# A hybrid encoder layer: the output projection's steps traced in a fixed order for every engine

## The chip, the core and the metric

The kernel runs on one core of a Trainium2 chip. The metric is device time in microseconds (us) of one execution; lower is better. The engines' short names are those of the profile: PE is TensorE's matmul, PEld its weight load, DVE VectorE, ACT ScalarE, POOL GpSimd, SP SyncE, which issues the DMAs.

## What is computed

One encoder layer on two sequences (1024 and 2048 rows of 1024 numbers, float32). The part that matters here is its end:

```python
u = rms_norm(h, norm_w); proj = u @ w_in
y_f = fourier(...) * silu(z_f)                      # 512 columns
y_s = (ssd_fwd + ssd_bwd + D * xs) * silu(z_s)      # 1536 columns, 4 groups of 384
yg = y_s.reshape(b, s, 4, 384)
yg = yg * rsqrt(mean(yg * yg, -1) + EPS)            # norm of each group
h = h + concatenate([y_f, y_s * ssd_norm_w], -1) @ w_out     # the output projection: 2048 -> 1024
h = h + (p @ w_ple_in) * sigmoid(h @ w_ple_gate)             # the last stage
return rms_norm(h, final_norm_w)
```

## The kernel before

Four stages follow each other: the input projection with the state space part, the Fourier part, the output projection, the last stage. The change is in the output projection (lines 1153 to 1264).

**Steps.** The 3072 rows are 24 chunks of 128 (eight each of the blocks P, S1 and S2), taken two at a time: 12 pairs. The 2048 inputs are split in two passes p of 1024. So there are 24 steps n, pair by pair, first pass 0 and then pass 1; each adds its part to the residual rows, which lie in memory between the passes (Hd). Between the passes, behind step 11, the weights are replaced (`product_weights`, lines 850 to 861: per product one load, four ACT casts, four DVE subtractions).

**One step.** A step multiplies a 2 x 2 arrangement of 128 x 512 blocks by the weights with seven products, in a Strassen-like scheme (P1, P2, P6, P5, P7, P4, P3 in that order, lines 1215 to 1238). Each product is 12 matmuls of 512 columns (line 1104), since each operand is split into a rounded part and a rest, and three of the four combinations count. Its operands A11, A12, S2, S1, S3, A22, S4 are made in `halves` (1066 to 1097): differences s3, s1, s2, s4 on DVE (L1080), the rounded part `ah` on ACT (L1074), the rest `al` on DVE (L1075). The products accumulate in PSUM: X takes P1, then P6, then P7 on top; Y takes P2; Z takes P5, then P3; W takes P4. Between P1 and P6, P6 and P7, and P7 and the next P1, ACT copies X out (`kept`, L1113, tile `pu`, called p1, u2, u3), and the next product on X waits for it. Each output quarter is then added to the residual tile `ht` by DVE out of PSUM (L1218) and by POOL from `pu` (L1219).

**Preparing a step.** The two y tiles of a step are loaded (L1173). For pairs of block S1 (n = 4 to 7 and 16 to 19) a correction comes first: 12 small matmuls `po` (L1185), four DVE multiplications into the tile `big` (L1186), two POOL additions into y (L1190). Then the group norm: ACT squares (L865, tile `sq`, one buffer), POOL sums each half in two additions (L866, L867) into `rs`; ACT rounds `rs` into `sh` (L871), POOL writes the rest (L872), PE sums over the partitions with two matmuls `pb` (L874), ACT takes Ln and Exp, each behind a table load (L875, L876). POOL then scales the two y tiles (L880). y has four buffers, `ht` four, the differences three, `ah` and `al` seven each.

**What sets the order.** The program traces, for every n, the first half of preparing step n + 2 (`prepare`), then the rest of preparing step n + 1, then the products of step n. The scheduler, with its own model of durations, sets from the dependencies which instruction each engine takes next. So the seven products of a step are interleaved with those of its neighbours, and every step has its own order. At run time each engine takes its instructions strictly in the order that was set.

Of the kernel before, what the change touches and what calls it, by code (L numbers as in the profile page):

```python
# [18 lines left out]
P = 128  # L19
# [37 lines left out]
def tile_hybrid_encoder(ctx: ExitStack, tc: tile.TileContext, a):  # L57
# [787 lines left out]
    def weight_tiles(pool, name):  # L845
        return [pool.tile([P, 4, 512], F32R, tag=f"w{x}{name}", name=f"w{x}{name}") for x in "hl"]
# [16 lines left out]
    def squares(y, sq, rs):  # L863

        S.activation(sq, y.rearrange("p (r k) l -> p r k l", r=2)[:, :, 1:4, :], AF.Square)  # L865
        G.tensor_tensor(rs, sq[:, :, 0, :], sq[:, :, 1, :], op=ALU.add)  # L866
        G.tensor_tensor(rs, rs, sq[:, :, 2, :], op=ALU.add)  # L867

    def group_rstd(sh, pb, rs):

        S.copy(sh[:, 0], rs)  # L871
        G.tensor_tensor(sh[:, 1], rs, sh[:, 0].bitcast(F32), op=ALU.subtract)  # L872
        for j in range(2):
            T.matmul(pb, lhsT=ones_r, rhs=sh[:, j], start=(j == 0), stop=(j == 1))  # L874
        S.activation(rs, pb, AF.Ln, bias=eps4, scale=1.0 / 384.0)  # L875
        S.activation(rs, rs, AF.Exp, scale=-0.5)  # L876

    def group_scale(y, rs):
        ssd = y.rearrange("p (r k) l -> p r k l", r=2)[:, :, 1:4, :]
        G.tensor_tensor(ssd, ssd, rs.unsqueeze(2).broadcast_to([P, 2, 3, P]), op=ALU.mult)  # L880

    with ExitStack() as ph:
# [63 lines left out]
        for step, (seq, f) in enumerate(order):  # L946
# [58 lines left out]
            if last:  # L1005
                for q in range(2):
                    pb = fpr.tile([P, 2, P], F32, tag="pm", name="pb")
                    sq = fp.tile([P, 2, 3, P], F32, tag="Uo", bufs=1, name="sq")
                    sh = fp.tile([P, 2, 2, P], F32R, tag="traw", name="sh")
                    rs = fp.tile([P, 2, P], F32, tag="fold0", name="rs")  # L1010
                    squares(y_first[:, q], sq, rs)
                    group_rstd(sh, pb, rs)
                    group_scale(y_first[:, q], rs)

# [84 lines left out]
    def product(ps, A, W, op, name, first=True):  # L1099
        (ah, al), (wh, wl) = A[op], W[name]  # L1100
        i = 0
        for k in range(4):
            for at, wt in ((ah, wh), (ah, wl), (al, wh)):
                T.matmul(ps, lhsT=at[:, k, :], rhs=wt[:, k, :], start=(first and i == 0), stop=(i == 11),  # L1104
                         skip_group_check=not first)
                i += 1
# [45 lines left out]

    with ExitStack() as ph:
        yp = ph.enter_context(tc.tile_pool(name="yp", bufs=1, **R_))
        hbs, behind = [], []
# [6 lines left out]
        def prepare(p, i):  # L1162

            ys, hts, rss = [], [], []
            for q in range(2):
                bi, c = todo[2 * i + q]
                b = BLOCKS[bi]
                tk = slice(c * P, (c + 1) * P)
                if p == 0 and i == 0:
                    y = y_first[:, q]  # L1170
                else:
                    y = yp.tile([P, 8, P], F32, tag="y", bufs=4, name="y")
                    nc.sync.dma_start(y, Yd[bi][:, 8 * p:8 * p + 8, tk])  # L1173
                ys.append(y)
                if b["n"] == "S1":

                    if not behind:
                        behind.append(ox.tile([P, 2, 8, P], F32, tag="big", name="big"))
                    ct, zb = behind[0][:, q, 0:2, :], behind[0][:, q, 2:8, :]
                    nc.sync.dma_start(ct, CTd[:, 2 * p:2 * p + 2, tk])  # L1180
                    nc.sync.dma_start(zb, ZSd[:, 6 * p:6 * p + 6, tk])
                    for g in range(2):
                        po = mps.tile([P, 3, P], F32, tag="sm", bufs=3, name="po")
                        for j in range(3):
                            T.matmul(po[:, j, :], lhsT=hbs[-1][:, 3 * g + j, :], rhs=ct[:, g, :], start=True, stop=True)  # L1185
                        V.tensor_tensor(zb[:, 3 * g:3 * g + 3, :], po, zb[:, 3 * g:3 * g + 3, :], op=ALU.mult)  # L1186
            for q in range(2):
                if BLOCKS[todo[2 * i + q][0]]["n"] == "S1":
                    ssd = ys[q].rearrange("p (r k) l -> p r k l", r=2)[:, :, 1:4, :]
                    G.tensor_tensor(ssd, ssd, behind[0][:, q, 2:8, :].rearrange("p (r k) l -> p r k l", r=2), op=ALU.add)  # L1190
                if p == 0 and i == 0:
                    continue
                if q == 0:
                    rs = yp.tile([P, 4, P], F32, tag="rs", bufs=2, name="rs")
                rss.append(rs[:, 2 * q:2 * q + 2])
                sq = yp.tile([P, 2, 3, P], F32, tag="sq", bufs=1, name="sq")
                squares(ys[q], sq, rss[q])
            if rss:
                sh = yp.tile([P, 2, 4, P], F32R, tag="sh", bufs=1, name="sh")
                pb = mps.tile([P, 4, P], F32, tag="sm", bufs=3, name="pb")  # L1200
                group_rstd(sh, pb, rs)

            def rest():
                for q in range(2):
                    if rss:
                        group_scale(ys[q], rss[q])
                    bi, c = todo[2 * i + q]
                    b = BLOCKS[bi]
                    r0 = b["t0"] + c * P
                    hts.append(residual(Hd[bi * NCH + c] if p else a["x"][b["seq"]][r0:r0 + P, :]))  # L1210
                quarter = lambda q, r: (lambda: ys[q][:, 4 * r:4 * r + 4, :])
                return halves(quarter(0, 0), quarter(0, 1), quarter(1, 0), quarter(1, 1)), hts
            return rest

        def outputs(i, W, A, hts):
            def add(q, ns, ps):
                h = hts[q][:, ns]
                V.tensor_tensor(h, ps, h, op=ALU.add)  # L1218
                return lambda t: G.tensor_tensor(h, h, t, op=ALU.add)  # L1219

            X, Y, Z, X2 = bank("X"), bank("Y"), bank("Z"), bank("W", bufs=2)
            product(X, A, W, "A11", "P1")
            p1 = kept(X)
            product(Y, A, W, "A12", "P2")
            add(0, N0, Y)(p1)
            product(X, A, W, "S2", "P6", first=False)
            u2 = kept(X)
            product(Z, A, W, "S1", "P5")
            more = add(1, N1, Z)
            product(X, A, W, "S3", "P7", first=False)  # L1230
            u3 = kept(X)
            more(u3)
            product(X2, A, W, "A22", "P4")
            add(1, N0, X2)(u3)
            product(Z, A, W, "S4", "P3", first=False)
            add(0, N1, Z)(u2)
            for q, (bi, c) in enumerate(todo[2 * i:2 * i + 2]):
                nc.sync.dma_start(Hd[bi * NCH + c], hts[q])

        ready = prepare(0, 0)()  # L1240
        ld = product_weights(0, NAMES[3:4], W)
        with tc.issue_after(ld.ins):
            coming = prepare(0, 1)
        ld = product_weights(0, NAMES[4:], W)
        with tc.issue_after(ld.ins):
            incoming(0)
        steps = [(p, i) for p in range(2) for i in range(NP)]
        for n, (p, i) in enumerate(steps):
            cur, after = ready, coming
            with tc.issue_after(ld.ins):  # L1250
                if n + 2 < len(steps):
                    if steps[n + 2] == (1, 0):
                        incoming(1)
                    coming = prepare(*steps[n + 2])
                if n + 1 < len(steps):
                    ready = after()
                else:
                    ph.close()
                    q4 = ctx.enter_context(tc.tile_pool(name="q4", bufs=1, **R_))
                    ready = turned(0)  # L1260
            outputs(i, W, *cur)
            if i == NP - 1:
                W = {}
                last_w = product_weights(p + 1, NAMES, W)


    wph = ox.tile([P, 2, DM], F32R, tag="big", name="wph")
# [123 lines left out]
```

## Time and profile before

| | us |
|---|---|
| median of 3 runs (2935.85 to 2945.36) | 2937.86 |
| the profiled execution | 2937.68 |
| its span | 2935.9 |
| PE busy in the span | 2806.0 (96%) |
| DVE, ACT, POOL busy | 2148.7, 1454.0, 1497.0 |
| output projection, first matmul | 2015.5 |
| last stage, first product | 2593.2 |

A PE row counts as busy until its modelled end, and matmuls overlap; how full PE is shows in the idle time before its rows and in the distance between their starts. "PEclk" is the clock that PE was granted, 1.00 being full speed. In a row of the timeline, the number in brackets is the idle time of the engine before it, and behind the arrow is what ended it.

### The profile page before, as it was taken

The page shows a single profiled execution, that of the slowest core. Times are in us where ns is not written, and L with a number is a line of the kernel's source. Part 1 is how long each engine was busy: PE and PEld are TensorE (multiplying, and loading weights), DVE is VectorE, ACT ScalarE, POOL GpSimd, SP SyncE. Part 2 cuts the span into 40 slices and gives each one's busy share as a digit, 9 for nine tenths or more (in the row PEclk, how much of TensorE's full clock was granted, in tenths as well). Part 3 has the DMA queues.
Part 4 walks back from the last instruction along what each step waited for, and adds up shares of the span by engine and source line. Part 5 has one row for each costly group of instructions (what it writes and reads, how often), then busy time and mean ns, then how long its engine had stood idle before and what let it go on. Part 6 is the DMA issues. An engine that isn't in the chain of part 4 may idle for free.

```text
span 2935.9 us, 46306 instructions
## 1 busy us (share of the span) xinstructions
PE 2806.0 (96%) x17206; PEld 2550.2 (87%) x17206; DVE 2148.7 (73%) x3364; ACT 1454.0 (50%) x3008; POOL 1497.0 (51%) x1091
## 2 busy tenths in 40 slices
PE   6999999999999999999999999788998899989998
PEld 6999999999999999999999999776776677768887
DVE  3787777687778686778787776796767876776665
ACT  4545465443545564445444444345555645555554
POOL 1255656542567777643656655455777577610000
PEclk9999999999999999999999999889999999999999
DMA  3244565462465665544455554466453654451221
GB/s 96 88 146 150 166 187 166 125 185 79 127 192 165 200 189 159 160 123 117 144 161 157 154 159 132 151 231 227 144 173 127 229 167 141 158 198 67 96 96 63
DMA packets 327997, 440.09 MB, mean 150 GB/s; under 512 B 19824, under 2 KB 250932, under 8 KB 323932
## 3 DMA queue, kind: packets, MB, share of 16 engines
q1 hardware_dynamic: 327484, 436.08, 47.1%
q8 instruction: 136, 2.23, 0.3%
q10 hardware_dynamic: 288, 1.05, 0.1%
q14 instruction: 89, 0.73, 0.1%
HBM read 328.41 MB, written 109.71 MB: 149 GB/s over the span
## 4 chain that ended last, share of the span: by engine, by line
PE 73%; DVE 7%; POOL 6%; issue 5%; DMA 5%; ACT 4%; SPq 0%; POOLq 0%; DVEq 0%; ACTq 0%
PE ps L361 41%; PE X L1104 7%; PE Z L1104 4%; PE po L648 4%; PE pst L606 3%; PE pd L574 3%; PE W L1297 2%; PE Y L1104 2%; DMA y<-Yd 2%; PE ptt L421 1%; DVE s L1080 1%; DVE al L1075 1%; PE W L1104 1%; PE pr L1028 1%; POOL wl L190 1%
## 5 line engine op out<-in xcount | busy, mean ns | idle before, releaser
L361 PE MATMUL ps<-uh,wh 128*128 128x342 f32 (+1 forms) x2880 | 955.8, 332 | 11.4 <-ACT uh L267 8.2
L361 PE MATMUL ps<-ul,wh 128*128 128x342 f32 (+1 forms) x2880 | 920.6, 320 | 2.5 <-DVE ul L268 2.5
L361 PE MATMUL ps<-uh,wl 128*128 128x342 f32 (+1 forms) x2880 | 922.2, 320 | 0.4 <-POOL wl L190 0.4
L190 POOL TENSOR_TENSOR wl<-wr,wh 128x1024 fp32r<-128x1024 f32 x120 | 296.4, 2470 | 659.3 <-ACT wh L189 658.1
L361 PEld LDWEIGHTS ps<-uh,wh 128*128 128x128 f32 x2880 | 545.6, 189 | 35.0 <-issue 15.8
L361 PEld LDWEIGHTS ps<-ul,wh 128*128 128x128 f32 x2880 | 548.5, 190 | 4.2 <-DVE ul L268 3.5
L361 PEld LDWEIGHTS ps<-uh,wl 128*128 128x128 f32 x2880 | 545.1, 189 | 1.2 <-POOL wl L190 1.1
L558 ACT ACTIVATE R<-R,lb 128x128 f32<-128x128 f32 x1152 | 352.8, 392 | 16.9 <-POOL R L549 16.9
L549 POOL TENSOR_SCALAR_AFFINE_SELECT R<-R 128x512 f32<-128x512 f32 x288 | 275.7, 980 | 6.8 <-DMA R<-ROWd 6.8
L586 POOL TENSOR_TENSOR xw<-xm,wd 128x512 f32<-128x512 f32 x144 | 189.5, 1327 | 136.3 <-ACT xm L423 110.8
L617 DVE SCALAR_TENSOR_TENSOR H<-H,cd,pst 128x64 f32<-128x64 f32 x888 | 182.6, 274 | 102.2 <-PE pst L606 100.0
L367 ACT COPY raw<-ps 128x342 f32<-128x342 f32 x180 | 79.1, 439 | 340.6 <-PE ps L361 339.7
L1104 PE MATMUL X<-whP,ah 128*128 128x512 f32 x480 | 196.7, 410 | 14.1 <-ACT pu L1113 8.4
L402 DVE SCALAR_TENSOR_TENSOR xT<-raw,cvt,xT 128x1024 f32<-128x1024 f32 x144 | 195.5, 1358 | 2.6
L1104 PE MATMUL X<-wlP,ah 128*128 128x512 f32 x480 | 194.5, 405 | 1.6 <-DVE wlP L859 1.6
L1104 PE MATMUL X<-whP,al 128*128 128x512 f32 x480 | 193.6, 403 | 2.4 <-DVE al L1075 2.4
L1219 POOL TENSOR_TENSOR ht<-ht,pu 128x512 f32<-128x512 f32 x96 | 150.4, 1578 | 72.3 <-ACT pu L1113 46.6
L652 DVE TENSOR_TENSOR y<-y,yt 128x512 f32<-128x512 f32 (+1 forms) x144 | 161.4, 1121 | 5.0
L272 ACT ACTIVATE zT<-ps 128x342 f32<-128x342 f32 (+1 forms) x108 | 49.1, 455 | 220.7 <-PE ps L361 220.4
L1075 DVE TENSOR_TENSOR al<-s,ah 128x512 fp32r<-128x512 f32 x144 | 137.7, 981 | 26.5 <-ACT ah L1074 26.0
L565 DVE TENSOR_TENSOR R<-R,cb 128x512 f32<-128x512 f32 x144 | 148.5, 1031 | 5.0
L651 DVE TENSOR_TENSOR yt<-po,er 128x512 f32<-128x512 f32 (+1 forms) x144 | 91.2, 633 | 75.9 <-PE po L648 67.7
(266 smaller groups left out, 5772.8 us busy)
## 6 DMA issues: line engine op xcount, KB each, us to landing
R<-ROWd SPq DMA_DIRECT2D x144, 512.0 KB
wr<-in_w_in SPq DMA_DIRECT2D x120, 512.0 KB
er<-EXPd SPq DMA_DIRECT2D x144, 256.0 KB
Hd<-ht SPq DMA_DIRECT2D x48, 512.0 KB
ht<-Hd SPq DMA_DIRECT2D x48, 512.0 KB
y<-Yd SPq DMA_DIRECT2D x46, 512.0 KB
wlP<-WSd SPq DMA_DIRECT2D x21, 1024.0 KB
Yd<-y SPq DMA_DIRECT2D x72, 256.0 KB
```

Of the source, the lines that this page charges most:

```text
L190: G.tensor_tensor(wl, raw, wh.bitcast(F32), op=ALU.subtract)
L361: T.matmul(ps[:, :n], lhsT=wt[:, kt, :], rhs=ut[:, kt, :n], start=(i == 0), stop=(i == 3 * KT - 1))
L402: V.scalar_tensor_tensor(dst, raw[:, k:k + TB], cvt[:, 20 * k + ct:20 * k + ct + 1], dst, op0=ALU.mult, op1=ALU.add)
L549: G.affine_select(out=R, in_=R, pattern=[[0, 2], [0, 2], [sgn, P]], compare_op=ALU.is_ge, fill=NEG, base=0, channel_multiplier=-sgn)
L558: S.activation(R[:, h, d, c, :], R[:, h, d, c, :], AF.Exp, bias=self.B.lb[:, 2 * p + c, hc + h:hc + h + 1])
L565: V.tensor_tensor(E[0], E[0], cb.unsqueeze(1).broadcast_to([P, 2, 2 * P]), op=ALU.mult)
L586: G.tensor_tensor(xw, self.xm[c4].rearrange("p c (h e) -> p c h e", h=2), col(self.B.wd[:, c4:c4 + 4, hc:hc + 2]).broadcast_to([P, 4, 2, 6 ...
L617: V.scalar_tensor_tensor(dst[:, e], H[d][:, cc, e], B.cd[:, cc, hc + h:hc + h + 1], pst[:, c, e], op0=ALU.mult, op1=ALU.add)
L652: V.tensor_tensor(y[:, cr], y[:, cr], t[:, cr], op=ALU.add)
L1075: V.tensor_tensor(al, src, ah.bitcast(F32), op=ALU.subtract)
L1104: T.matmul(ps, lhsT=at[:, k, :], rhs=wt[:, k, :], start=(first and i == 0), stop=(i == 11), skip_group_check=not first)
L1219: return lambda t: G.tensor_tensor(h, h, t, op=ALU.add)
```

## The change

The output projection's loop is written as a class `Step` with small pieces (load, correct, square, sum, root, scale, each operand, each addition, store), and a function `run(n)` that traces the pieces of three steps at once: the products of step n (`c`), the operands of step n + 1 (`d`), the correction and squares of step n + 2 (`e`), and the store of step n - 1 (`b`). Steps 1 to 22 are traced under `tc.manual_schedule()`, in which the order of every engine and of the DMA queue is the order of the text. Step 0 and step 23 are left to the scheduler. `group_rstd` is split: its ACT rounding and POOL subtraction become `group_parts`. The new weights between the passes are asked for and split inside step 11's text, product by product. Every engine has the same instructions as before, each as often; only their order differs.

```diff
-        ready = prepare(0, 0)()
...
-        for n, (p, i) in enumerate(steps):
-            cur, after = ready, coming
-            with tc.issue_after(ld.ins):
...
-                    coming = prepare(*steps[n + 2])
-                if n + 1 < len(steps):
-                    ready = after()
...
-            outputs(i, W, *cur)
+        def run(n, newer=None):
+            c = all_[n]
+            b = all_[n - 1] if n else None
+            d = all_[n + 1] if n + 1 < len(steps) else None
+            e = all_[n + 2] if n + 2 < len(steps) else None
...
+            c.operand(6)
+            product(X, c.A, W_, "A11", "P1")
+            if d is not None and not d.first and n:
+                d.rooted()
             p1 = kept(X)
+            if e is not None:
...
+                e.rows()
+            if d is not None:
+                d.scaled(0)
+                d.scaled(1)
+            product(Y, c.A, W_, "A12", "P2")
+            asked(0)
+            c.add(0, N0, Y)
+            c.plus(0, N0, p1)
+            if b is not None:
+                b.stored()
+            product(X, c.A, W_, "S2", "P6", first=False)
+            asked(1)
             u2 = kept(X)
+            if d is not None:
+                d.operand(0)
+            product(Z, c.A, W_, "S1", "P5")
+            asked(2)
+            c.add(1, N1, Z)
+            if d is not None:
+                d.operand(1)
+                d.operand(2)
+            if e is not None:
+                e.correct(0)
+            parted(0)
+            product(X, c.A, W_, "S3", "P7", first=False)
+            asked(3)
             u3 = kept(X)
+            c.plus(1, N1, u3)
+            if e is not None:
+                e.correct(1)
+                e.squared(0)
+            if d is not None:
+                d.operand(3)
+            parted(1)
+            product(X2, c.A, W_, "A22", "P4")
+            asked(4)
+            c.add(1, N0, X2)
+            c.plus(1, N0, u3)
+            if d is not None:
+                d.residuals()
+                d.operand(4)
+            if e is not None:
+                e.squared(1)
+            parted(2)
+            product(Z, c.A, W_, "S4", "P3", first=False)
+            asked(5)
+            c.add(0, N1, Z)
+            if e is not None:
+                e.summed()
+            if d is not None:
+                d.operand(5)
+            c.plus(0, N1, u2)
+            parted(3)
+            if newer is not None:
+                asked(6)
+                for k in range(4, 7):
+                    parted(k)
...
+        with tc.manual_schedule():
+            for n in range(1, len(steps) - 1):
+                run(n, newer=W if n == NP - 1 else None)
```

`rooted` is the two pb matmuls, Ln and Exp; `summed` is the ACT and POOL parts of `sh`. `operand(k)` makes, for k = 0 to 6: A11 and s3; s1 and A12; s2 and S2; S1; S3; A22; s4 and S4. `asked` and `parted` do something in step 11 alone. Behind `two` stand, as before, `S.copy(ah, src)` and then DVE's subtraction into `al`.

Three places show what moves. First ACT, around the Ln and Exp of a step of the first pass, before; the three casts from s tiles are S2, S1 and S3, the cast of y is A22, and the last is S4:

```order
L871 CAST sh<-rs 128x512
L1074 CAST ah<-s_22983 128x512
L1074 CAST ah<-s_22981 128x512
L1074 CAST ah<-s_22979 128x512
L1113 COPY pu<-X 128x512
L875 ACT_TABLE_LOAD
L875 ACTIVATE rs<-pb,eps_117 128x512
L1074 CAST ah<-y 128x512
L876 ACT_TABLE_LOAD
L876 ACTIVATE rs<-rs 128x512
L865 ACTIVATE sq<-y 128x768
L1074 CAST ah<-s_23005 128x512
```

and ACT of the change, from the second squares of step n + 2 over the step's end; the cast of y behind `sh` is A22, that of s_22944 is S4, both of step n + 1:

```order
L865 ACTIVATE sq<-y 128x768
L870 CAST sh<-rs 128x512
L1238 CAST ah<-y 128x512
L1238 CAST ah<-s_22944 128x512
L877 ACT_TABLE_LOAD
L877 ACTIVATE rs<-pb,eps_117 128x512
L878 ACT_TABLE_LOAD
L878 ACTIVATE rs<-rs 128x512
L1116 COPY pu<-X 128x512 x2
L1238 CAST ah<-y 128x512 x2
L1238 CAST ah<-s_23030 128x512
L1116 COPY pu<-X 128x512
```

Ln stood ahead of the casts of A22 and S4 and now stands behind both; the copy of X (p1, the first of the `x2`) stands behind Exp; the copy u3 (the last row) stands behind the cast of S2.

Second DVE, a step of the second pass before, from the addition of P4 (W) over that of P3 (Z) to P2's of the next step (Y); s_24836 and s_24834 are s2 and s1, s_24858 is s4:

```order
L1218 TENSOR_TENSOR ht<-W,ht 128x512
L1075 TENSOR_TENSOR al<-y,ah 128x512
L1218 TENSOR_TENSOR ht<-Z,ht 128x512
L1075 TENSOR_TENSOR al<-s_24836,ah 128x512
L1075 TENSOR_TENSOR al<-s_24834,ah 128x512
L1080 TENSOR_TENSOR s_24858<-y,s_24836 128x512
L1218 TENSOR_TENSOR ht<-Y,ht 128x512
```

and of the change, the whole stretch from P5's addition (first row) to P2's of the next step; s_24881, s_24887, s_24866 and s_24968 are s1, s2, s3 and s4:

```order
L1266 TENSOR_TENSOR ht<-Z,ht 128x512
L1232 TENSOR_TENSOR s_24881<-y 128x512
L1239 TENSOR_TENSOR al<-y,ah 128x512
L1232 TENSOR_TENSOR s_24887<-s_24881,y 128x512
L1239 TENSOR_TENSOR al<-s_24887,ah 128x512
L1239 TENSOR_TENSOR al<-s_24881,ah 128x512
L1266 TENSOR_TENSOR ht<-W,ht 128x512
L1239 TENSOR_TENSOR al<-s_24866,ah 128x512
L1266 TENSOR_TENSOR ht<-Z,ht 128x512
L1239 TENSOR_TENSOR al<-y,ah 128x512
L1232 TENSOR_TENSOR s_24968<-y,s_24887 128x512
L1239 TENSOR_TENSOR al<-s_24968,ah 128x512
```

The differences s1 and s2 now stand behind P5's addition, and s4 behind P3's addition and the rest of A22.

Third POOL in a step whose step n + 2 needs the correction, before:

```order
L1219 TENSOR_TENSOR ht<-ht,pu 128x512 x2
L880 TENSOR_TENSOR y<-y,rs 128x2x384 x2
L1190 TENSOR_TENSOR y<-y,big 128x2x384
L1219 TENSOR_TENSOR ht<-ht,pu 128x512
L866 TENSOR_TENSOR rs<-sq 128x256
L867 TENSOR_TENSOR rs<-rs,sq 128x256
L1190 TENSOR_TENSOR y<-y,big 128x2x384
L1219 TENSOR_TENSOR ht<-ht,pu 128x512
L866 TENSOR_TENSOR rs<-sq 128x256
L867 TENSOR_TENSOR rs<-rs,sq 128x256
L872 TENSOR_TENSOR sh<-rs,sh 128x512
```

and in the change:

```order
L882 TENSOR_TENSOR y<-y,rs 128x2x384 x2
L1270 TENSOR_TENSOR ht<-ht,pu 128x512
L1203 TENSOR_TENSOR y<-y,big 128x2x384
L1270 TENSOR_TENSOR ht<-ht,pu 128x512
L1203 TENSOR_TENSOR y<-y,big 128x2x384
L866 TENSOR_TENSOR rs<-sq 128x256
L867 TENSOR_TENSOR rs<-rs,sq 128x256
L1270 TENSOR_TENSOR ht<-ht,pu 128x512
L866 TENSOR_TENSOR rs<-sq 128x256
L867 TENSOR_TENSOR rs<-rs,sq 128x256
L871 TENSOR_TENSOR sh<-rs,sh 128x512
L1270 TENSOR_TENSOR ht<-ht,pu 128x512
```

Both corrections now stand with the addition of u3 between them ahead of all the sums; before, the first half's sums stood between them.

More of the change, by code (lines that the diff above doesn't have):

```diff
@@ L1187, in prepare @@
[L1187 to L1192, printed above, removed]
+                    self.ys.append(y)
+                    if self.corrected:
+                        if q == 0:
+                            self.big = ox.tile([P, 2, 8, P], F32, tag="big", name="big")
+                        nc.sync.dma_start(self.big[:, q, 0:2, :], CTd[:, 2 * p:2 * p + 2, tk])
+                        nc.sync.dma_start(self.big[:, q, 2:8, :], ZSd[:, 6 * p:6 * p + 6, tk])
@@ L1230, in outputs @@
-            product(X, A, W, "S3", "P7", first=False)
-            u3 = kept(X)
[L1232 to L1238, printed above, removed]
-        ready = prepare(0, 0)()
+            if e is not None:
+                if steps[n + 2] == (1, 0):
+                    incoming(1)
+                e.rows()
```

198 lines of the change are left out of this document (138 added, 60 removed).

## Prediction, made before the changed kernel was run

> **What bounds the kernel now.** I first read the busy time of the output projection against that of the last stage. Columns: length, then busy time of PE, PEld, DVE, ACT and POOL with their counts, granted clock, DMA share, GB/s.
>
> ```profile
> 2016.00:2592.00 576.00, 531.12 (x2257) 414.19 (x2255) 429.80 (x452) 302.44 (x463) 397.45 (x275) 0.97 0.53 179
> 2600.00:2900.00 300.00, 298.98 (x1405) 242.78 (x1403) 191.87 (x309) 159.89 (x310) 0.00 (x0) 1.00 0.24 82
> ```
>
> The last stage is full; the projection has 45 us without a matmul and a lower clock. Next, what a full PE would need, from the first and the last row of P1 of step 0 and the rows of W, the tile of P4:
>
> ```profile
> 2015.51 0.39 PE L1104 MATMUL X<-whP,ah 128*128 128x512 f32 x1
> ...
> 2018.30 0.39 PE L1104 MATMUL Y<-whP,ah 128*128 128x512 f32 x1
> ```
> ```profile
> L1104 PE MATMUL W<-whP,ah x96: 390/396/737, 2037.4 to 2570.4; 128*128 128x512 f32 x96
> ```
>
> Twelve matmuls take 2.79 us, 0.2325 each. A step has 84 and two for pb: 20.0 us; with the correction's 12 small ones about 20.7. From the first W row to the last are 23 steps and most of a product, 533 us: about 23.0 us a step. So some 3 us a step is lost, near 65 in all. The chain of waits names what for:
>
> ```profile
> PE X L1104 <- ACT pu L1113: 8.4, 5, 3.3
> PE Z L1104 <- DVE ht L1218: 7.8, 4, 3.7
> PE W L1104 <- ACT ah L1074: 7.7, 6, 2.9
> PE X L1104 <- ACT ah L1074: 5.7, 3, 3.0
> PE Y L1104 <- DVE al L1075: 4.8, 5, 3.5
> ```
>
> (total us, times, longest): no one cause, but operands and copies that come late now and then. And waits cost twice:
>
> ```profile
> 2182.83 0.39 PE L1104 MATMUL Z<-whP,al 128*128 128x512 f32 x1
> 2185.65 0.50 PE L1104 MATMUL X<-whP,ah 128*128 128x512 f32 x1 [2.43 <-ACT pu L1113]
> ```
> ```profile
> 2186.50:2189.80 3.30, 3.30 (x9) 2.56 (x8) 2.08 (x2) 1.14 (x2) 3.30 (x3) 0.50 0.02 5
> ```
>
> After 2.43 us idle, PE had half its clock for 3.3 us, 1.65 us of work lost.
>
> **What the change does to the path.** Nothing is removed or added; it is all order. The gain to be had is those 65 us. What it may cost is seen by following the new order round one step, from P6's start to the next P6's start: each link below is the next instruction that must end first, by data or by its engine's queue. Durations (shortest/median/longest ns) of the links:
>
> ```profile
> L1219 POOL TENSOR_TENSOR ht<-ht,pu x96: 1270/1715/1801, 2026.3 to 2591.9; 128x512 f32<-128x512 f32 x96
> L866 POOL TENSOR_TENSOR rs<-sq x46: 718/747/1243, 2028.2 to 2532.9; 128x256 f32<-128x256 f32 x46
> L867 POOL TENSOR_TENSOR rs<-rs,sq x46: 731/1069/1199, 2029.1 to 2533.7; 128x256 f32<-128x256 f32 x46
> L1190 POOL TENSOR_TENSOR y<-y,big x16: 1832/2018/2310, 2091.2 to 2444.4; 128x768 f32<-128x768 f32 x16
> L1075 DVE TENSOR_TENSOR al<-s,ah x96: 674/693/2893, 2017.0 to 2568.7; 128x512 fp32r<-128x512 f32 x96
> L1075 DVE TENSOR_TENSOR al<-y,ah x69: 674/1081/2337, 2047.3 to 2563.8; 128x512 fp32r<-128x512 f32 x69
> L1080 DVE TENSOR_TENSOR s<-y x46: 677/1227/2336, 2050.1 to 2548.5; 128x512 f32<-128x512 f32 x46
> L1080 DVE TENSOR_TENSOR s<-s,y x23: 681/693/1820, 2053.0 to 2550.4; 128x512 f32<-128x512 f32 x23
> L1080 DVE TENSOR_TENSOR s<-y,s x23: 676/1665/1787, 2056.2 to 2558.4; 128x512 f32<-128x512 f32 x23
> L1186 DVE TENSOR_TENSOR big<-po,big x32: 540/545/559, 2070.9 to 2439.9; 128x384 f32<-128x384 f32 x32
> L1218 DVE TENSOR_TENSOR ht<-Z,ht x48: 673/678/693, 2032.3 to 2580.3; 128x512 f32<-128x512 f32 x48
> L1074 ACT CAST ah<-s x95: 600/617/628, 2015.4 to 2567.7; 128x512 fp32r<-128x512 f32 x95
> ```
>
> ACT's own run of them stands in the timeline of before, with POOL's part of sh:
>
> ```profile
> 2128.20 0.62 ACT L871 CAST sh<-rs 128x512 fp32r<-128x512 f32 x1
> 2128.73 0.58 ACT L1113 COPY pu<-X 128x512 f32<-128x512 f32 x1
> 2129.33 1.28 ACT L875 ACT_TABLE_LOAD   x1
> 2131.43 0.69 ACT L875 ACTIVATE rs<-pb,eps 128x512 f32<-128x512 f32 x1 [0.82 <-PE pb L874]
> 2132.14 1.28 ACT L876 ACT_TABLE_LOAD   x1
> 2133.43 0.63 ACT L876 ACTIVATE rs<-rs 128x512 f32<-128x512 f32 x1
> ```
> ```profile
> 2128.90 1.58 POOL L872 TENSOR_TENSOR sh<-rs,sh 128x512 fp32r<-128x512 f32 x1 [0.73 <-ACT sh L871]
> ```
>
> POOL began 0.08 us after ACT's 2128.82: I take 0.08 per hand-over.
>
> 1. P6 and P5: 24 x 0.2325 and the last one's end, 5.8.
> 2. DVE: P5's addition, s1, the rest of A12, s2. POOL has done its scaling and p1's addition by then and stands still, so the shortest rows: 0.67 + 0.68 + 0.67 + 0.68 = 2.7. With all medians 3.7.
> 3. ACT: cast of S2, then the copy u3, which stands behind it: 0.62 + 0.58 = 1.2.
> 4. POOL: u3's addition, sums of the first half, u3's second addition, sums of the second half. Shortest 2 x 1.27 + 2 x 1.45 = 5.4, medians 2 x 1.72 + 2 x 1.82 = 7.1. DVE's rests of S1 and S3 lie beside the first three; I take 6.3.
> 5. ACT: sh, cast of A22: 1.2.
> 6. DVE: rest of A22, s4. POOL's sh and u2's addition lie beside both, so the medians 1.08 + 1.67 = 2.75; shortest 1.35.
> 7. ACT: cast of S4 0.62, table load 1.28, Ln to Exp's end 2.63, copy p1 0.58: 5.1. Then P6.
>
> With seven hand-overs (0.5) the ring takes **25.6 us**, at shortest 23.2, with all medians 27.2: longer than PE's 20.0 by 5.6, and longer than the 23.0 of before. PE waits twice in it: at the second pb, behind POOL's sh (sh is there 18.2 us after P6's start, the 72 matmuls to pb take 16.7: 1.4), and at P6 behind p1 (4.2). P2 is all that PE has to do meanwhile.
>
> In the eight steps that correct step n + 2 (n = 2 to 5, 14 to 17), link 3 is followed by the rest of S2 (0.69), two multiplications into big (1.09) and the first correction (1.85) instead of the copy (0.58), and POOL has the second correction (2.0) in its queue ahead of the sums: 5.1 more, **30.7**; shortest 28.0, medians and longest about 33.
>
> The clock: a wait of 4.2 us is longer than those above, so P6 and P5, which are in the ring, would run at half clock for a while: up to 1.65 more per ring. Part of such a window may fall on P7, where PE has slack; I take half, 0.85: 26.4 and 31.5.
>
> The Trainium skill ("TensorE: Matmul & The Clock Gate", section "What's actually happening") has the clock halve only after an idle window of about 3.4 us. The rows above show it after 2.43. For the wait of 4.2 both say the same. With the shortest durations the wait at P6 is about 2.7: by the page the clock then stays and the result is the low end below; by the rows it halves and the result is some 35 us above that end.
>
> Step 11 puts new weights into the same queues: four casts ahead of u3 (2.5) and 16 between the casts of A22 and S4 (9.9): 25.6 + 12.4 = 38. The loads themselves are covered if they land within that time.
>
> DMAs, by the chain that ended last (start, length):
>
> ```profile
> 2058.54 5.98 DMA y<-Yd
> ...
> 2259.18 4.27 DMA y<-Yd
> ```
>
> y of step n + 2 is asked for when s4 of step n has been read, near Ln, and squared 13 us later at the earliest; its waits before are of 4 to 6 us, so I cost that at nothing. A later landing would lengthen link 4.
>
> Sum. Rings run from P6 of step 1 to P6 of step 22: 21, of which 8 with correction, one with weights, 12 plain: 12 x 26.4 + 8 x 31.5 + 38 = 607 us.
>
> ```profile
> 2058.64 0.40 PE L1104 MATMUL X<-whP,ah 128*128 128x512 f32 x1
> ...
> 2593.17 0.79 PE L1104 MATMUL X<-whP,ah 128*128 128x512 f32 x1 [1.14 <-ACT ah L1074]
> ```
>
> Before, P6 of step 1 began at 2058.6. In step 1 Ln already stands behind S4's cast; I put P6 5 us later (0 to 8), at 2064. Behind P6 of step 22 come 60 + 84 matmuls, 33.5 us, and about 2 of waits. The last stage's first product: 2064 + 607 + 35 = 2706, against 2593.2. The last stage is full and stays as it is. So +113 us on the profiled 2937.7 (0.2 under the median): **3050**. With the shortest rows and full clock: 12 x 23.2 + 8 x 28.0 + 33 = 535, from 2059: 2627, +34, 2972. With medians and 1.65 everywhere: 12 x 28.8 + 8 x 34.6 + 42 = 664, from 2066: 2766, +173, 3111.
>
> **Rivals.** *Forecast*, rings with collisions and some half clock: 3010 to 3110, 0.52. *Lock-step without collisions*: in a fixed order DVE and POOL settle so that they rarely meet, and the clock stays: 2970 to 3010, 0.29. For it: long idle times of POOL in a long ring. Against: links 4 and 6 have the other engine's work beside them by the order itself. *Slower still*, a y load that lands late or two half-clock windows per step: above 3110, 0.11.
>
> *Faster*: the ring doesn't close, since the table load and Ln get to ACT before S4's cast is due; then PE alone paces a step. Place: link 7. It decides from a ring of 20.9 downward (20.0 and 0.9 for P6 behind Ln, Exp and p1 alone, 3.8 after pb against P2's 2.8). Then 12 x 20.9 + 8 x 21.6 + 33 = 457, and 2059 + 457 + 34 = 2550: -43, 2895. For it: PE's waits of before all come from such accidents of order. Against: ACT's queue as written, and 23.2 as the shortest ring. 0.05. *Nothing to measure*: the rings come out at 23.5 or so on average, what before takes: 0.03; the corrections' 28.0 speak against it.
>
> **How the numbers follow.** 3050 is the forecast's middle. From 2970 to 3105 lie the forecast, the lock-step case and both ends of the unknown durations, 0.8. A measurement of this kernel can tell about 0.3% (9 us) from no change: faster 0.05, same 0.03, slower 0.92.
>
> **What would show it.** Right: PE's waits led by X behind ACT's pu, some 4 us in each of 22 steps, then pb behind POOL's sh; W rows 26 to 27 us apart, 31 in steps 3 to 6 and 15 to 18; half-clock windows about once a step; the last stage's first product near 2706. Wrong: W rows under 23 apart; pu waits under 1 us; POOL waiting on DMA for y; the loss lying in the last stage or in step 12 alone.

## The result, and the profile after

The changed kernel takes 3062.52 us (median of 4 runs, 3060.26 to 3065.62) against 2939.33 for the kernel before: a ratio of 1.0426 (95% interval 1.0412 to 1.044). It is slower by 123 us; 3050 was predicted. The profiled execution took 3065.62 with a span of 3063.8.

The busy time by stage, in the columns of the prediction's first fence (length; PE, PEld, DVE, ACT, POOL; granted clock, DMA share, GB/s):

```profile
2016.00:2718.00 702.00, 573.61 (x2260) 442.58 (x2261) 346.58 (x442) 297.37 (x451) 364.40 (x272) 0.90 0.43 144
2720.00:3020.00 300.00, 294.66 (x1370) 238.02 (x1369) 198.52 (x319) 164.13 (x317) 6.29 (x3) 1.00 0.29 100
```

The output projection, which took 576 us, takes 702 with the same instructions, and its clock went from 0.97 to 0.90. DVE and POOL are busy for less time than before (346.6 for 429.8, 364.4 for 397.5). PE's rows take longer at the lower clock (573.6 for 531.1), but most of the loss is standing still: 128 us without a matmul, where it was 45. The waits of PE in that stage (total us, times, longest):

```profile
PE X L1107 <- ACT pu L1116: 77.0, 21, 11.0
PE pb L876 <- ACT sh L870: 25.1, 10, 5.6
PE pb L876 <- POOL sh L871: 18.3, 22, 0.9
```

Instead of many causes with a few waits each there are now three places. Two return step by step: pb waits for POOL's sh in all of the 22 steps traced in the fixed order, and P6 waits for the copy in 21 of them: 4.07 or 4.08 us at the end of a plain ring, 11.0 at the new weights, but only 1.4 to 2.7 at the end of a ring with a correction. The third, pb behind ACT's sh, is 1.7 us in each of the eight correcting steps and 5.6 twice, in step 1 and at the new weights. One plain step as each engine ran it: PE first, from one P6 to the next, then the links in the order of the prediction (DVE, ACT, POOL, ACT, DVE, ACT).

```profile
2244.58 0.50 PE L1107 MATMUL X<-whP,ah 128*128 128x512 f32 x1 [4.07 <-ACT pu L1116]
...
2264.34 0.50 PE L876 MATMUL pb<-sh,ones_r 128*128 128x512 f32 x1 [0.85 <-POOL sh L871]
...
2271.71 0.50 PE L1107 MATMUL X<-whP,ah 128*128 128x512 f32 x1 [4.08 <-ACT pu L1116]
```
```profile
2252.03 0.69 DVE L1266 TENSOR_TENSOR ht<-Z,ht 128x512 f32<-128x512 f32 x1 [0.37 <-PE Z L1107]
...
2253.84 0.69 DVE L1232 TENSOR_TENSOR s<-s,y 128x512 f32<-128x512 f32 x1
```
```profile
2254.56 0.62 ACT L1238 CAST ah<-s 128x512 fp32r<-128x512 f32 x1 [3.70 <-DVE s L1232]
2255.08 0.58 ACT L1116 COPY pu<-X 128x512 f32<-128x512 f32 x1
```
```profile
2255.74 1.32 POOL L1270 TENSOR_TENSOR ht<-ht,pu 128x512 f32<-128x512 f32 x1 [6.77 <-ACT pu L1116]
2257.02 1.22 POOL L866 TENSOR_TENSOR rs<-sq 128x256 f32<-128x256 f32 x1
2258.31 1.20 POOL L867 TENSOR_TENSOR rs<-rs,sq 128x256 f32<-128x256 f32 x1
2259.47 1.30 POOL L1270 TENSOR_TENSOR ht<-ht,pu 128x512 f32<-128x512 f32 x1
2260.72 0.75 POOL L866 TENSOR_TENSOR rs<-sq 128x256 f32<-128x256 f32 x1
2261.55 0.74 POOL L867 TENSOR_TENSOR rs<-rs,sq 128x256 f32<-128x256 f32 x1
```
```profile
2262.32 0.62 ACT L870 CAST sh<-rs 128x512 fp32r<-128x512 f32 x1 [1.93 <-POOL rs L867]
2262.85 0.61 ACT L1238 CAST ah<-y 128x512 fp32r<-128x512 f32 x1
2266.62 0.62 ACT L1238 CAST ah<-s 128x512 fp32r<-128x512 f32 x1 [3.16 <-DVE s L1232]
2267.26 1.28 ACT L877 ACT_TABLE_LOAD   x1
...
2271.09 0.57 ACT L1116 COPY pu<-X 128x512 f32<-128x512 f32 x1
```
```profile
2263.50 1.34 DVE L1239 TENSOR_TENSOR al<-y,ah 128x512 fp32r<-128x512 f32 x1 [2.38 <-ACT ah L1238]
2264.76 1.77 DVE L1232 TENSOR_TENSOR s<-y,s 128x512 f32<-128x512 f32 x1
```

Each link begins within 0.1 us of the end of the link before, and the last row releases the next P6: 27.13 us from P6 to P6. The waits of 0.85 and 4.08 are PE's two places. The clock behind the long wait, as a window of the same columns:

```profile
2246.00:2248.00 2.00, 2.00 (x6) 1.52 (x6) 0.00 (x0) 0.00 (x0) 2.00 (x2) 0.50 0.38 104
```

### The profile page after: what moved, and what is told of

The parts are those of the page before. It is cut to its first block, busy times and chain, and to the rows that moved or that the text cites. A ratio compares the mean times of both kernels' runs of the same rounds, so it can differ in the third digit from the quotient of the medians.

```text
span 3063.8 us, 46116 instructions
## 1 busy us (share of the span) xinstructions
PE 2849.1 (93%) x17206; PEld 2578.8 (84%) x17206; DVE 2073.1 (68%) x3364; ACT 1454.4 (47%) x3008; POOL 1469.0 (48%) x1091
## 5 line engine op out<-in xcount | busy, mean ns | idle before, releaser
L1107 PE MATMUL X<-whP,ah 128*128 128x512 f32 x480 | 206.4, 430 | 79.2 <-ACT pu L1116 77.6
L1239 DVE TENSOR_TENSOR al<-y,ah 128x512 fp32r<-128x512 f32 x69 | 63.2, 917 | 232.9 <-ACT ah L1238 232.9
L1107 PE MATMUL X<-wlP,ah 128*128 128x512 f32 x480 | 202.4, 422 | 1.5 <-DVE wlP L859 1.5
L1107 PE MATMUL X<-whP,al 128*128 128x512 f32 x480 | 201.6, 420 | 0.9 <-DVE al L1239 0.9
L1270 POOL TENSOR_TENSOR ht<-ht,pu 128x512 f32<-128x512 f32 x96 | 139.3, 1452 | 124.6 <-ACT pu L1116 97.3
L1107 PEld LDWEIGHTS X<-whP,ah 128*128 128x128 f32 x480 | 96.8, 202 | 112.6 <-ACT pu L1116 88.3
```

## The experiments

All are edits of the changed kernel. The first nine were run once each; the kernel before, on the same chips, took 2933.1 us (beside the first four), 2938.4 (the next three) and 2939.4 (the two behind them). The theory is the prediction's ring. The rivals are that PE's own pace with the half clock sets the step, that the other engines do, by their own work or by slowing each other, or that the loss has nothing to do with the order.

### S4's cast late

```diff
-            c.operand(6)
             product(X, c.A, W_, "A11", "P1")
...
             p1 = kept(X)
+            c.operand(6)
```

> The change with one piece of text moved: s4 and the operand S4 are made behind the copy p1 instead of ahead of P1, so that on ACT Ln no longer stands behind S4's cast. Theory (one ring through all queues, closed at ACT by A22's cast, s4, S4's cast, table load, Ln, Exp, p1, P6): in the change's trace sh ends 18.4 us after P6's start; Ln then waits only for the second pb matmul, 1.9 us after sh, and P6 comes at 18.4 + 1.9 + 2.6 + 0.6 = 23.6 after the last P6; both PE waits fall under 1.8 us, so the half-clock window should go too: 22.0 to 23.7 a plain step against 27.1, 26.5 to 28.3 a correcting one against 30.8. Total 2962 to 2997 us. Rival 1 (POOL's chain from u3 to sh, with pb behind it, is the limit, and where Ln stands is of no matter): 27 us a step as before, 3045 or more. Rival 2 (any order fixed by hand loses the interleaving of the products, whatever its details): 3040 or more.

2968.62 us, 94 us less than the changed kernel (88 when each is set against the kernel before on its own chip), within the theory's interval. The waits of PE in the stage:

```profile
PE pb L876 <- ACT sh L870: 28.1, 10, 7.6
PE pb L876 <- POOL sh L871: 18.4, 22, 0.9
PE X L1107 <- ACT pu L1116: 10.9, 13, 6.0
```

The wait for the copy fell from 77.0 us to 10.9, and the other two stayed. A plain step takes 21.90 us (W rows at 2250.95 and 2272.85), with no half clock in it. So the ring was closed through links 6 and 7.

### PE kept busy in the wait

14 matmuls of 512 columns into a PSUM tile that nobody reads are put behind P2 in nine plain steps: extra work, in time that PE otherwise waits.

```diff
...
+                for k in range(14):
+                    T.matmul(idle, lhsT=c.A["A12"][0][:, k % 4, :], rhs=W_["P2"][0][:, k % 4, :], start=True, stop=True)
             product(X, c.A, W_, "S2", "P6", first=False)
```

> The change with 14 more matmuls of 512 columns between P2 and P6 in the plain steps 7 to 10, 12, 13 and 19 to 21, into a PSUM tile that nothing reads. They fill 3.3 us of the 4.07 us that PE waits there. Theory: the wait stays where it is, but PE keeps its full clock, so that the ring with P6 and P5 in it gets 1.65 us shorter: 25.5 us from step to step in eight of those steps (all but 12) instead of 27.1, and about 13 us less in all, 3050, although PE does more. Rival (the half clock is only a sign of the waits and lies in slack, or more matmuls ahead of P6 delay it): 27.1 or more a step, 3062 to 3070.

3052.17 us, the span 13.4 us below that of the changed kernel, though PE does more. Of these, 4.5 us lie ahead of the first step (first W row at 2035.04 for 2039.55) and have nothing to do with the filling; from the first to the last W row it is 663.0 us for 671.5. P6's first row, and the first of P7 24 matmuls later:

```profile
2241.64 0.50 PE L1107 MATMUL X<-whP,ah 128*128 128x512 f32 x1 [0.81 <-ACT pu L1116]
...
2247.34 0.39 PE L1107 MATMUL X<-whP,ah 128*128 128x512 f32 x1
```

P6 and P5 take 5.70 us here. In the changed kernel P7 begins at 2251.83, 7.25 after P6. The 1.55 between them is the half clock, and eight of the nine filled steps (all but the one behind the new weights) take 25.57 us, less by as much than the 27.11 of a plain step in the changed kernel. They make 13 us together; the other steps took 4.6 more. So P6 and P5 are in the ring, and the half clock falls on them in full.

### The same text, ordered by the scheduler

```diff
-        with tc.manual_schedule():
-            for n in range(1, len(steps) - 1):
...
+        for n in range(1, len(steps) - 1):
```

> The change's new text without the fixed order: steps 1 to 22 go through the scheduler as step 0 does. Theory (the loss is in the order that was fixed, not in the new pieces): the scheduler finds its way round the ring as in the kernel before, 23 us a step, 2920 to 2965 in all, with no wait of P6 behind p1 that comes back in every step. Rival 3 (the order of the text, as the scheduler's priority, or the pieces themselves, are what costs): 3000 or more.

2959.19 us, within the interval expected: some 100 of the 123 us are the fixed order's. It is still 26 above the kernel before on that chip. One row of its waits tells of some of that:

```profile
PE Z L1107 <- ACT whP L858: 9.9, 1, 9.9
```

In the kernel before this wait for the first weights is 2.0 us in two times; so the other text costs 8 us in step 0 alone. Another 14.6 lie between the first and the last W row (542.7 us for 528.1 before); at which waits was not followed up.

### The copy p1 ahead of the rooted sums

```diff
+            p1 = kept(X)
             if d is not None and not d.first and n:
                 d.rooted()
-            p1 = kept(X)
```

> The change with two pieces of text swapped: the copy p1 stands ahead of pb, Ln and Exp on ACT. Theory: p1 then waits for S4's cast alone, the table loads, Ln and Exp leave the ring at P6 (3.9 us), but Exp now comes 3.8 us after P6 instead of ahead of it, and the scaling, s3 and P5's addition move back: P6 to P6 by 24.0 us, or 25.2 if the longer wait at pb halves the clock under P2. Correcting steps about 28.5 against 30.8. Total 2990 to 3030 us. Rival 1 (POOL's chain with pb behind it): pb stays where it is, 27 us a step, 3050 or more. Should PE's waits have nothing to do with ACT's queue: 3062.

3032.26 us, 2 above the interval given, nearer to the theory than to the rival, but a smaller gain than expected. Ln and Exp no longer stand ahead of P6, so P6 starts on time; but they have left one ring for another. ACT's and DVE's rows:

```profile
2262.26 0.63 ACT L878 ACTIVATE rs<-rs 128x512 f32<-128x512 f32 x1
...
2264.84 1.14 ACT L1238 CAST ah<-y 128x512 fp32r<-128x512 f32 x2 [1.00 <-POOL y L882]
...
2287.65 0.63 ACT L878 ACTIVATE rs<-rs 128x512 f32<-128x512 f32 x1
```
```profile
2265.50 1.68 DVE L1239 TENSOR_TENSOR al<-y,ah 128x512 fp32r<-128x512 f32 x1 [4.35 <-ACT ah L1238]
2267.10 1.78 DVE L1232 TENSOR_TENSOR s<-y 128x512 f32<-128x512 f32 x1
2268.80 0.68 DVE L1266 TENSOR_TENSOR ht<-Z,ht 128x512 f32<-128x512 f32 x1
```

P5's addition (ht<-Z) has no idle time ahead of it any more: it stands behind A11's rest and s3, which wait for the scaling, which waits for Exp. From Exp to Exp 25.4 us: the ring is closed through the scaling instead of through P6 and P5, and it is about as long.

### u3's second addition late

```diff
             c.add(1, N0, X2)
-            c.plus(1, N0, u3)
...
                 d.operand(5)
+            c.plus(1, N0, u3)
             c.plus(0, N1, u2)
```

> u3's second addition on POOL is moved behind the parts of the sums (its first one stays). Theory (the ring of seven links sets the step): link 4 loses one addition of 1.3 us, so a plain step goes from 27.1 us to 25.8 and a correcting one loses as much; 21 steps by 1.3 us are 27 us, so some 3035 us (3025 to 3045) where the kernel before takes 2939. The waits of P6 behind the copy p1 in the plain steps shrink from 4.07 to about 2.8 us. Rival (POOL has time to spare, and the casts on ACT or the share of the memory port set the step by themselves): the addition only changes its place, 3055 us or more, the waits stay at 4.07.

3066.48 us: the expectation failed. The rival's number came out, and so did its sign: the waits of P6 stayed at 4.08 us, and the one at pb fell from 0.85 to 0.67. But the rows give another reason than its time to spare on POOL. ACT's and POOL's rows of the second half of the squares:

```profile
2260.17 0.85 ACT L865 ACTIVATE sq<-y 128x768 f32<-128x768 f32 x1 [2.12 <-POOL rs L867]
```
```profile
2261.09 0.74 POOL L866 TENSOR_TENSOR rs<-sq 128x256 f32<-128x256 f32 x1 [0.96 <-ACT sq L865]
```

`sq` has one buffer, so ACT can square the second half only when POOL has summed the first, and POOL needs that square next. The addition of 1.30 us had covered that round trip of 0.96. Without it POOL waits, and link 4 is only 0.3 shorter; the steps take 26.9, or 27.5 where a little more half clock falls on them. This reading is from the trace; a second `sq` buffer, which would test it, wasn't tried.

### A22's cast ahead of the sums' cast

```diff
+            if d is not None:
+                d.operand(5)
             if e is not None:
                 e.summed()
-            if d is not None:
-                d.operand(5)
```

> Two calls swapped: A22's cast and its rest stand ahead of the sums' cast sh, everything else as in the changed kernel, S4 at its place ahead of P1 too. Theory (the ring): link 6 and A22's cast, 3.03 and 0.62 us, leave the ring, because VectorE can then make the rest of A22 and s4 while ScalarE waits for POOL's sums; the wait of P6 falls from 4.07 us to under 1, and with it the half clock of 1.65 us a step: 27.1 less 3.65 less 1.65 is 21.8 us a plain step, as with S4 late, so some 2975 us (2962 to 3005). Rival (that S4 stands ahead of p1 on ScalarE is what costs, wherever A22 stands): the wait stays above 3 us, 3040 us or more.

2978.67 us, with plain steps of 22.24 us: within the theory's interval, 84 us gained by one swap of two neighbours. S4 stands at its place ahead of P1; what counted was that DVE's 3 us stood between POOL's sums and Ln.

### The order redone, in three goes

First go: y is asked for ahead of P1, p1 and S4's cast stand ahead of the rooted sums, s4's difference is made a step earlier, A22 ahead of the sums' cast, u3's second addition late, the last three weights' casts spread over the next step (in this and the next two diffs the `if` lines and smaller moves are left out).

```diff
+            e.rows()
             product(X, c.A, W_, "A11", "P1")
             p1 = kept(X)
...
+            c.operand(6)
...
             d.rooted()
...
             d.operand(5)
+            d.last()
             e.summed()
             c.plus(1, N0, u3)
```

> All of the order redone by the ring's reading, still fixed by the program: y asked for first; behind P1 the copy p1, then S4's cast (its difference made at the end of the step before) and then the rooted sums; half of the squares ahead of P7; A22's cast and s4 ahead of the sums' cast, u3's second addition behind it; the new weights' last four parts spread over the next step. Theory (nothing but the chain of engines from one P6 to the next held PE; without it a step is PE's own 20.0 us and the two products of pb): 20.5 us in a plain step, 22 to 23 in a correcting one, some 6 us lost at the weights: 490 us for the 23 steps where the kernel before takes 508, so some 2918 us (2895 to 2940). Rival (the engines beside PE slow each other so much in any order that a step can't come under e1's 21.9 us): 2960 us or more.

2964.09 us: 46 more than expected. Plain steps take 21.76 us each, 1.3 more than expected. The larger part of the 46, some 33 us, lies in the eight correcting steps, which take 24.4 to 28.8 us where 22 to 23 were expected, with PE waiting 1.6 to 1.8 us at pb in each; what makes sh late there was not worked out. The ACT rows of a plain step show what sets that one:

```profile
2242.70 1.14 ACT L1238 CAST ah<-y 128x512 fp32r<-128x512 f32 x2 [0.51 <-POOL y L882]
2248.07 0.62 ACT L1238 CAST ah<-s 128x512 fp32r<-128x512 f32 x1 [4.22 <-DVE s L1232]
2248.59 0.84 ACT L865 ACTIVATE sq<-y 128x768 f32<-128x768 f32 x1
```

The square of step n + 2 needs nothing of step n + 1, but it stands behind S2's cast, which waits 4.22 us for DVE. Exp, scaling, A11, s1, s2, S2, squares, sums, pb, Exp are a new ring of 21.8 us. The number was the rival's, but in the next two goes the order alone takes it lower. Second go, against the first: the squares ahead of S2's cast, the scaling ahead of p1's addition, the sums' parts ahead of A22's cast, the new weights' casts spread over two steps; and the same with pb and the rooted sums behind P2:

```diff
             c.add(1, N1, Z)
+            e.squared(0)
             e.correct(1)
             d.operand(1)
+            e.squared(1)
             d.operand(2)
-            e.squared(0)
```

> The order redone once more, still fixed by the program. In the last redone order every plain step took 21.76 us, because ScalarE's squares stood behind S2's cast, and so the rooted sums, the scaling, A11, s1, s2, S2's cast, the squares, their sums and pb made a new ring. Here both squares stand ahead of S2's cast, the sums' parts ahead of A22's, the scaling ahead of p1's addition on POOL, the new weights' casts are spread over two steps, and the rooted sums of the first step come behind P2. Theory (a chain from one step to the next sets the pace, and no other limit lies between it and PE's own work): plain steps of 20.4 to 20.8 us, correcting ones 22 to 25, some 2918 us (2900 to 2940), below the kernel before. Rival (VectorE and POOL slow each other on their shared port, so a step of 21.8 us is what any order gives): plain steps stay at 21.5 us or more, 2950 us or more.

> As the squares-first order, but the two products of pb and the rooted sums stand behind P2 instead of behind P1 in every step, so that the sums have 2.8 us more before PE asks for them, and the scaling ends 2.8 us later. Theory: the waits of pb behind sh in the correcting steps (1.7 us, and the half clock behind each) are gone, and the plain steps stay at PE's pace; 0 to 15 us less than the squares-first order. Rival (the scaling was on the path, a ring again): plain steps grow by up to 2.8 us, 2940 us or more.

2945.99 and 2944.08 us. The first is above its interval by 6 us and below the rival's 2950; its plain steps are between 20.6 and 22.4, so the ring of 21.8 was no limit of the engines. The second is 2 us less, too little for two single runs to tell from nothing. The waits of pb for sh in the correcting steps went, as expected (in the whole stage 13.7 us behind POOL and 3.2 behind ACT in the first form), but the waits for the copy grew from 15.2 to 22.7 us, and the plain steps, now 21.2 to 21.8, are 0.3 longer on average. So the rival's sign, plain steps that grow and 2940 or more, came out as well. The longest waits of the second form:

```profile
PE X L1107 <- ACT pu L1116: 22.7, 24, 2.5
```

The copy u3 now stands behind the second square, which waits for POOL. Third go, on the second of the two: u3's copy ahead of that square and of S2's cast, u3's additions in POOL's waits, p1's addition ahead of the scaling.

```diff
             u3 = kept(X)
+            c.plus(1, N1, u3)
+            e.squared(1)
+            d.operand(2)
...
             c.add(1, N0, X2)
+            c.plus(1, N0, u3)
+            e.summed()
```

> The order with the rooted sums behind P2, changed where its trace still shows a chain: in the correcting steps P1 waited 1.4 to 2.1 us for the copy u3, which stood on ScalarE behind the second square, and POOL (some 22.6 us of work and 3 us of waits in a step of 25.8) set the pace; in the plain steps P1 waited 0.4 us for the same copy. Here u3's copy stands ahead of the second square and of S2's cast, u3's additions fill POOL's wait for that square and for the sums' cast, and p1's addition fills its wait for the rooted sums. Theory (what is left is the order, each wait with a place): plain steps 20.4 to 20.9 us, correcting ones 22.5 to 24.5, so 12 to 30 us less than the 2944 us of that order: some 2922 us (2910 to 2935), 0.2 to 1 per cent below the kernel before. Rival (the engines' shared memory port is the limit by now): 2940 us or more, no faster than the kernel before.

2931.71 us (12 runs, 2929.40 to 2933.07) against 2936.49 (17 runs) of the kernel before: a ratio of 0.9984 (95% interval 0.9975 to 0.9992), within the interval expected, 10 us above its middle; the gain of 0.16 per cent is just short of the 0.2 to 1 forecast, and the rival's 2940 did not come. Two neighbouring W rows and PE's largest wait that is left:

```profile
2249.02 0.40 PE L1107 MATMUL W<-whP,ah 128*128 128x512 f32 x1
...
2269.70 0.39 PE L1107 MATMUL W<-whP,ah 128*128 128x512 f32 x1
```
```profile
PE pb L876 <- POOL sh L871: 17.5, 18, 5.0
```

A plain step takes 20.7 us, 0.7 above PE's own 20.0. The correcting ones take 22.7 to 25.7, a little above what was expected, and the two steps around the new weights 35.3 and 25.5: some 20 us more than two plain ones, the largest loss at one place (the eight correcting steps together lose 26 us against their 20.7 each). The whole is 5 us faster than the scheduler's order.

The runs in one table: time and the distance of two W rows in plain steps.

| kernel | us | plain step, us |
|---|---|---|
| changed kernel | 3062.5 | 27.1 |
| u3's second addition late | 3066.5 | 26.9 to 27.6 |
| PE kept busy (filled steps) | 3052.2 | 25.6 |
| p1 ahead of the rooted sums | 3032.3 | about 24.4 and 26.5, mostly in turn |
| A22 ahead of the sums' cast | 2978.7 | 22.2 |
| S4's cast late | 2968.6 | 21.9 |
| redone, first go | 2964.1 | 21.8 |
| the same text, ordered by the scheduler | 2959.2 | no fixed step |
| redone, second go (two forms) | 2946.0, 2944.1 | 20.6 to 22.4, 21.2 to 21.8 |
| redone, third go | 2931.7 | 20.7 |
| kernel before | 2933.1 to 2939.4 | no fixed step; 23.0 on average, corrections among them |

## Why the prediction was right, and where its terms were off

**The ring.** The seven links were put at 25.6 us. Measured from the rows above, without the half clock: P6 and P5 5.8; DVE 2.5 (2.7 expected); ACT 1.1 (1.2); POOL 6.55 (6.3); ACT 1.14 (1.2); DVE 3.03 (2.75); ACT 5.04 (5.1); with the hand-overs 25.5. That the ring is the cause, and not only as long as the step, was shown by opening it at two places: S4's cast late and A22's cast early each take over 80 us out. The two waits of PE in it were about as said in a plain step, 0.85 at pb (1.4 expected) and 4.08 at P6 (4.2).

**The half clock.** This term was mis-sized. Half of 1.65 us a ring was taken, since some of a window might fall on P7. It fell on P6 and P5 in full: seven of the twelve plain rings took 27.1 us for the expected 26.4, the two behind the new weights 27.9 and 28.4; the filled wait shows that this is the clock. The other three begin with a P6 that waited 1.44 us or not at all. They had no half clock on P6 and P5 and took 25.5 us from P6 to P6: the ring as it was summed, in the changed kernel itself. The Trainium skill ("TensorE: Matmul & The Clock Gate", section "What's actually happening") gives the half clock after at least one idle window of about 3.4 us, and calls the window free-running. By that a wait of 4.2 us need not hold a whole window, so the prediction's "both say the same" read more out of the page than it states. And no wait of 3.4 us was needed here: two waits of 1.74 and 0.85 us, 3.1 us from the first's start to the second's end, were followed by half clock in all eight correcting steps of the kernel with S4's cast late. In one of them, the rows behind the waits stand 0.43 apart:

```profile
2137.93 0.49 PE L876 MATMUL pb<-sh,ones_r 128*128 128x512 f32 x1 [1.74 <-ACT sh L870]
2139.27 0.50 PE L876 MATMUL pb<-sh,ones_r 128*128 128x512 f32 x1 [0.85 <-POOL sh L871]
...
2141.42 0.63 PE L1107 MATMUL Y<-whP,ah 128*128 128x512 f32 x1
2141.84 0.63 PE L1107 MATMUL Y<-wlP,ah 128*128 128x512 f32 x1
```

A window that runs free would explain that like pairs of waits need not do it: in three of the eight correcting steps of the first redone order the clock stayed at full speed. In one of these the rows stand 0.23 apart:

```profile
2136.02 0.49 PE L876 MATMUL pb<-sh,ones_r 128*128 128x512 f32 x1 [1.68 <-ACT sh L870]
2137.38 0.50 PE L876 MATMUL pb<-sh,ones_r 128*128 128x512 f32 x1 [0.86 <-POOL sh L871]
...
2140.05 0.40 PE L1107 MATMUL Y<-wlP,ah 128*128 128x512 f32 x1
2140.28 0.39 PE L1107 MATMUL Y<-whP,al 128*128 128x512 f32 x1
```

**The correcting steps.** 31.5 us was put for each; by the W rows they take 29.7 to 31.7, and their rings from P6 to P6 30.2 to 32.3, 31.3 on average. But the sign that was named, some 4 us at P6 in every step, failed in them: PE waited 2.6 us at the two pb and then only 1.4 to 2.7 at P6. From the second pb to P6 it is 7.4 us as in a plain step (2150.04 to 2157.39, for 2264.34 to 2271.71), so this is ACT's link 7 as before; the half clock fell on P2, within that time, and filled the wait at P6. In the two rings that had P6 and P5 at full clock it took 30.2 us (30.7 put), in the other six 31.5 to 32.3. So the ring itself was half a us shorter and the half clock in it longer than put: the average came so close to 31.5 by luck.

**The new weights.** 38 us were put for that ring; it took 42.8 (P6 at 2353.04 and 2395.84). The rows of ACT, and one of DVE:

```profile
2377.64 8.41 ACT L1286 CAST whP<-wlP 128x512 fp32r<-128x512 f32 x16
2390.76 0.62 ACT L1238 CAST ah<-s 128x512 fp32r<-128x512 f32 x1 [4.71 <-DVE s L1232]
```
```profile
2379.32 10.80 DVE L1287 TENSOR_TENSOR wlP<-wlP,whP 128x512 fp32r<-128x512 f32 x16
```

The 16 casts are shorter than the 9.9 put for them, but S4's cast then waits 4.71 us for s4. The step that failed: only ACT's queue was counted, and DVE has 16 subtractions of the weights ahead of s4. Besides, this ring, too, has a P6 wait of 4.07 us and the half clock behind it (P7 7.25 us after P6), for which its 38 us had no term.

**The sum.** P6 of step 1 began at 2068.0 (2064 expected) and the 21 rings took 616 us (607), so the last stage began at 2717.1 (2706). It was said to stay as it is; it took 346.7 us for 342.7, with two waits of 2 us for operands in its first 25 us. These, less 2 us behind the last P6 (33 for 35), are the 15 us between the forecast and the profiled execution. By rings: the twelve plain ones 6 us more than put, the one with the weights 5 more, the correcting ones 1 less.

**The rivals.** Lock-step without collisions was half true: POOL's additions took 1.3 us in the ring, not the median 1.72, and the first links had the shortest rows. But A22's rest and s4 met POOL's sh and u2's addition in every step (1.34 and 1.77), and the clock did halve. The loads of y, costed at nothing, never held an engine in the ring.

## What to carry to other kernels

In a fixed order, follow one step from an instruction through data and queues to the same instruction of the next step: if that ring is longer than the busiest engine's work, it is the pace, whatever the engines' shares say. What belongs in a queue ahead of what is decided by who waits behind it: an instruction that waits for another engine blocks all the work behind it that was ready, so a swap of two neighbours was worth 84 us here. When one link is shortened, look for what it covered before counting the gain, and for the ring that is next.

## What the runs showed of the hardware

- TensorE's clock can halve after 2.6 us of waits split in two, and need not: the same pair (1.74 and 0.85 us; 1.68 and 0.86) was followed by half clock at one place and by full clock at another. In the kernel before, all eight waits of 2.3 to 3.7 us that PE had between its first and last W row were followed by half clock; of the changed kernel's five waits of 2.5 to 2.7 at P6 four were, and its three of 1.44 were not. Matmuls that nobody reads, put into a wait of 4.1 us, left 0.81 of it and kept the clock: a step was 1.55 us shorter.
- The mean of DVE's and POOL's instructions in that stage is 0.78 and 1.34 us in the fixed order of the change (346.58 by 442, 364.40 by 272), 0.95 and 1.45 in the scheduler's, 0.99 and 1.49 in the fastest order (row below). Among these three, the closer the steps are packed, the longer each instruction takes; short ones were no sign of a good order.

```profile
2016.00:2572.00 556.00, 516.59 (x2220) 405.48 (x2219) 427.81 (x431) 293.42 (x441) 406.43 (x272) 0.97 0.52 174
```
